# Moving the rearrangement of a latent convolution's data from its load and store to the producer's store and the consumer's load

## The chip, the cores and the metric

The kernel runs on one core of one Trainium2 chip. The metric is the device time of one execution in microseconds. TensorE (PE) multiplies matrices, VectorE (DVE), ScalarE (ACT) and GpSimd (POOL) work on tiles of 128 partitions, and SyncE (SP) issues all of this kernel's DMAs, in the order of one queue. Matrix products land in PSUM banks; everything between stages goes through DRAM buffers.

## The reference, cut to what matters

One layer of a backbone over 256 context tokens and 2048 latent tokens with 1024 channels. A normalised and modulated input is multiplied by one input projection. One part of its columns feeds a state-space scan; two others, `ga` and `gb`, feed the branch that matters here:

```python
def conformer_branch(ga, gb, conv_w, conv_b, ln_g, ln_b):
    h = ga * jax.nn.sigmoid(gb)
    h = depthwise_conv(h, conv_w, conv_b)   # 31 taps, per channel
    h = layer_norm(h, ln_g, ln_b)           # over the 1024 channels
    return jax.nn.silu(h)
```

The latent tokens lie on a grid of 32 rows by 64 columns, and the convolution runs along the rows (for each column and channel, 31 taps over 32 row positions). The context tokens are convolved along the sequence. Then `y_conf * silu(gsil)` and the scan's output are concatenated, multiplied by `w_out` (2048 x 1024), normalised, gated and added to the input.

## The kernel before, in words

The 2304 tokens are split in two halves (blocks of 256, 512, 512 and of 512, 512 tokens; block 0 is the context). All products are done three times with split operands (high times high, high times low, low times high), so TensorE has much to do. For each half the kernel runs, in this order: the columns of the scan's input (`xbc_phase`), then the units of `post`: eight `gab_unit`s, one for each group `j` of 128 channels, then the `silu_unit`s of the gates. Beside `post` run a scan over the tiles (`pass_a`) and, in the second half, the convolutions; generators are interleaved by hand (`interleave`, `merge`). On top of this a scheduler that simulates a time line lays out each engine's queue when the program is built, so the order within an engine need not be the written one; what is issued by one engine runs in its queue's order.

`gab_unit` makes `th`, the gated product of 128 channels by 256 or 512 tokens, in a buffer `ev` of which there are three, and stores it (L532) to `GL[j]`, one row a channel, token after token. Weights come through `next_w`, three units ahead.

`lat_conv` treats a group `j` of 128 channels. Its matmuls (L626) contract over 32 grid rows of 4 channels at once, so it wants the input as `x`: partition (channel mod 4, grid row), then channel group `g` and grid column. It loads that from `GL[j]` with four DMAs (L608), each run being 64 columns, 256 bytes. ScalarE expands the taps from `kd` into `kbuf` (`expand`, L614). VectorE gathers the result from PSUM into `vt` (named cvv in the profile; partition: one of two channel halves, grid column; then grid row and 64 channels). Two DMAs (L636) store it to `CVL`, one row a token, in runs of 64 channels, 256 bytes. There is one `x` buffer and one `vt` buffer.

The end of the kernel is the out-projection over 18 tiles of 128 tokens, latent tiles from the last to the first, then the two context tiles. For each tile: `conf_pre` (L1028) loads the convolution's result `n` (cn) of 128 tokens by 1024 channels (one buffer, L1030), takes the statistics (L1033) and normalises it; `conf_act` (L1041) transposes it on TensorE (L1049) and applies the activation; `ssd_pre` (L959) loads and combines the scan's parts (y, z, elb; L977 to L982), with GpSimd updating the carried state (L988, L989); `ssd_norm` and `ssd_scale` make its normalisation factor yr and yh, yl; `out_part` (L1069) runs 96 matmuls, and `finish` (L1085, L1089) scales the result, adds the input and stores it. The steps are written so that a tile's preparation lies between the matmuls of the tile before.

Of the kernel before, what the change touches and what calls it, by code (L numbers as in the profile page):

```python
# [17 lines left out]
P = 128  # L18
D = 1024
KT = D // P  # L20
NH = 16
HD = 64
NT = 18
NCTX = 2
LAT = 2048
# [42 lines left out]
def backbone_kernel(ctx, tc, xa, xt_in, cols, rows, wconv, conf_b, gp_row, bg_row, state0, w_mod, w_dt, w_in, w_out,  # L68
                    y_ctx, y_lat, new_state):
    nc = tc.nc  # L70
    V, S, G, T, DMA = nc.vector, nc.scalar, nc.gpsimd, nc.tensor, nc.sync
# [5 lines left out]
    def bank(tag, name):  # L77
        return psp.tile([P, 512], F32, tag=tag, name=name, bufs=3 if tag == "mm" else 5)

    def dram(name, shape):  # L80
        return drp.tile(shape, F32, tag=name, name=name)
# [1 line left out]
    XB = [dram(f"xb{h}", [NCT * P, n]) for h, n in ((0, N1), (1, N2))]  # L83
    HALO = dram("halo", [NCT, P, 130])
    ZS = [dram(f"zs{h}", [D, HT[h] * P]) for h in range(2)]
    GL = [dram(f"gl{j}", [P, NT * P]) for j in range(KT)]
    GS = [dram(f"gs{h}", [D, HT[h] * P]) for h in range(2)]
    CVC = dram("cvc", [NCTX * P, D])
    CVL = dram("cvl", [LAT, D])
    YP = [dram(f"yp{i}", [P, D]) for i in range(NT)]  # L90
    ST = [dram(f"st{i}", [P, D]) for i in range(NT)]
    LT = [dram(f"lt{h}", [HT[h] * 32, P]) for h in range(2)]
# [33 lines left out]
    def rstd_of(pool, ms, name):  # L126
        r = pool.tile([P, 1], F32, tag="rstd", name=name, bufs=4)
        G.tensor_tensor(r, ms, nhalf, ALU.pow)
        return r
# [39 lines left out]
    def ev(name):  # L169
        return evp.tile([P, 512], F32, tag="ev", name=name, bufs=3)  # L170
# [189 lines left out]
    def next_w():  # L360
        while len(wq) < 3 and wcols:
            wq.append(load_w(*wcols.pop(0)))
        return wq.pop(0)

    def mm_cm(ps, w, h):
        wh, wl = w
        hh, hl = h
        BN = hh.shape[2]
        for k in range(KT):
            T.matmul(ps[:, :BN], wh[:, k, :], hh[:, k, :], start=(k == 0), stop=False)  # L370
            T.matmul(ps[:, :BN], wh[:, k, :], hl[:, k, :], start=False, stop=False)  # L371
            T.matmul(ps[:, :BN], wl[:, k, :], hh[:, k, :], start=False, stop=(k == KT - 1))  # L372
            yield
# [146 lines left out]
    def gab_unit(half, j, hb):  # L520
        wb = next_w()
        wa = next_w()
        for b in ORDER[half]:
            BN, o = BNS[b], TOK[b]
            pg = bank("mm", f"gb{half}_{j}_{b}")
            yield from mm_cm(pg, wb, hb[b])
            th = ev(f"gth{half}_{j}_{b}")[:, :BN]
            S.activation(th, pg[:, :BN], AF.Tanh, scale=0.5)  # L528
            pa_ = bank("mm", f"ga{half}_{j}_{b}")
            yield from mm_cm(pa_, wa, hb[b])  # L530
            V.scalar_tensor_tensor(th, th, 1.0, pa_[:, :BN], ADD, MUL)  # L531
            DMA.dma_start(GL[j][:, o:o + BN], th)  # L532

    def silu_unit(half, c0, dst, j, hb, order=None):
        w = next_w()
# [36 lines left out]
    def ctx_conv(j, tile):  # L572
        g = tile(f"cg{j}")
        G.memset(g[:, 0:15], 0.0)
        G.memset(g[:, 271:286], 0.0)
        DMA.dma_start(g[:, 15:271], GL[j][:, 0:256])
        yield
        acc = g[:, 512:768]
        w0 = C_CONFW + j * CW
        V.tensor_scalar(acc, g[:, 0:256], cv[:, w0:w0 + 1], cfb2[:, j:j + 1], MUL, ADD)  # L580
        for t in range(1, CW):
            V.scalar_tensor_tensor(acc, g[:, t:t + 256], cv[:, w0 + t:w0 + t + 1], acc, MUL, ADD)  # L582
            if t % 3 == 0:
                yield
        ps = bank("ss", f"cps{j}")
        for t in range(2):
            T.transpose(ps[:, t * P:(t + 1) * P], acc[:, t * P:(t + 1) * P], ident)
        o = g[:, 768:1024]
        S.mul(o, ps[:, :256], 0.5)
        DMA.dma_start(CVC[:, j * P:(j + 1) * P].rearrange("(t p) c -> p t c", p=P),  # L590
                      o.rearrange("p (t c) -> p t c", c=P))
        yield


    def lat_conv(j, lp, kbuf):
        cbb = lp.tile([P, HD], F32, tag="cbb", name=f"cbb{j}", bufs=2)
        for h in range(2):
            c0 = j * P + h * 64
            DMA.dma_start(cbb[h * 64:(h + 1) * 64], conf_b[c0:c0 + 64].partition_broadcast(64))
        kd = lp.tile([P, 32, 32], F32, tag="kd", name=f"kd{j}", bufs=1)  # L600
        for c4 in range(4):
            src = bass.AP(tensor=wconv.tensor, offset=(j * 4 + c4) * 64 * 32, ap=[[32, 32], [1, 1024]])
            DMA.dma_start(kd[c4 * 32:(c4 + 1) * 32].rearrange("p r g -> p (r g)"), src)

        x = lp.tile([P, 32, 64], F32, tag="cx", name=f"cx{j}", bufs=1)
        src = GL[j][:, 256:].rearrange("(g c) (r w) -> c r g w", c=4, w=64)
        for c4 in range(4):
            DMA.dma_start(x[c4 * 32:(c4 + 1) * 32], src[c4])  # L608

        def expand(u):  # L610
            kt = kbuf[u % 2]
            for c4 in range(4):
                rs = slice(c4 * 32, (c4 + 1) * 32)
                S.copy(kt[rs, :, rs].rearrange("p (h q) r -> p h q r", h=2),  # L614
                       kd[rs].rearrange("p r (h u q) -> p u h q r", h=2, u=4)[:, u])

        vt = lp.tile([P, 32, HD], F32, tag="cvv", name=f"cvv{j}", bufs=1)
        yield
        expand(0)
        yield  # L620
        for u in range(4):
            kt = kbuf[u % 2]
            ps = bank("ss", f"cp{j}_{u}")
            for q in range(4):
                for h in range(2):
                    T.matmul(ps[h * 64:(h + 1) * 64, q * P:(q + 1) * P], x[:, h * 16 + u * 4 + q, :], kt[:, h * 4 + q, :],  # L626
                             start=True, stop=True)
            if u < 3:
                expand(u + 1)
            yield  # L630
            V.scalar_tensor_tensor(vt[:, ::-1, u * 16:(u + 1) * 16].rearrange("p r c -> p c r"),
                                   ps.rearrange("p (c r) -> p c r", r=32), 0.5,
                                   cbb[:, u * 16:(u + 1) * 16].unsqueeze(2).to_broadcast([P, 16, 32]), MUL, ADD)
        for h in range(2):
            c0 = j * P + h * 64
            DMA.dma_start(CVL[:, c0:c0 + 64].rearrange("(r w) c -> w r c", w=64), vt[h * 64:(h + 1) * 64])  # L636
        yield


# [222 lines left out]
    def post(half, nb):  # L862
        return chain([gab_unit(half, j, hb) for j in range(8)] + [silu_unit(half, Z0, ZS, j, hb) for j in range(8)]
                     + [silu_unit(half, GS0, GS, j, hb) for j in range(nb)])
# [31 lines left out]
    V.tensor_tensor(wd4[:, :, 1, :], wdr, wd4[:, :, 0, :].bitcast(F32), SUB)  # L896
    xbc_phase(0, first, hb, [hprep(2, hb), hprep(0, hb)], tails, dt_post(0))
    extra = chain([gate_rows()] + [ctx_conv(j, big) for j in range(4)])
    interleave(post(0, 6), merge(scan(range(9)), 68, extra, 9 + 4 * 13), 90 * 8)
    last = [silu_unit(0, GS0, GS, j, hb, (1, 2, 0)) for j in (6, 7)]  # L900
# [23 lines left out]
    blocks = post(1, 5)  # L924
    cg = lambda name: lp.tile([P, D], F32, tag="cg", name=name, bufs=2)
    extra = chain(f for j in range(4) for f in (lat_conv(2 * j, lp, kbuf), ctx_conv(j + 4, cg), lat_conv(2 * j + 1, lp, kbuf)))
    sc_ = scan(range(9, NT))
    run(take(blocks, 24))
# [98 lines left out]

    def conf_pre(i):  # L1028
        n = p2.tile([P, D], F32, tag="cn", name=f"cn{i}", bufs=1)
        DMA.dma_start(n, CVC[i * P:(i + 1) * P, :] if i < 2 else CVL[(i - 2) * P:(i - 1) * P, :])  # L1030
        bs = p2.tile([P, 12], F32, tag="bs", name=f"bs{i}", bufs=2)
        for h in range(2):
            V.bn_stats(bs[:, 6 * h:6 * h + 6], n[:, h * 512:(h + 1) * 512])  # L1033
        mv = p2.tile([P, 2], F32, tag="mv", name=f"mv{i}", bufs=2)
        V.bn_aggr(mv, bs)
        V.tensor_scalar(mv[:, 1:2], mv[:, 1:2], EPS, None, ADD)
        r = rstd_of(p2, mv[:, 1:2], f"cr{i}")
        V.tensor_scalar(n, n, mv[:, 0:1], r, SUB, MUL)
        return n
# [59 lines left out]
    i = order[0]  # L1099
# [9 lines left out]
    for b in range(2):  # L1109
        for n, u in enumerate(last):  # L1110
            run(take(u, 8))
            if b == 0 and n == 1:
                yr = ssd_norm(i, yz)
            if b == 1 and n == 0:
                ph_b[1].close()
                p2 = ph_1.enter_context(tc.tile_pool(name="p2", bufs=1))
                yh = ssd_scale(i, yr)
                nrm = conf_pre(i)
# [11 lines left out]
    for a, i in enumerate(order):  # L1130
# [10 lines left out]
        if not last:  # L1141
            n = conf_pre(nxt)
# [76 lines left out]
```

## Time and profile before

| | |
|---|---|
| Runs of the kernel before | 1885.21 us median of 3 (1884.33 to 1887.44) |
| Profiled execution | 1890.22 us, span 1888.5 us, 26833 instructions |
| Mean granted clock of TensorE | 0.989 |
| DMA | 375.29 MB, mean 199 GB/s; queue busy 63.9% of 16 engines' span |
| Packets under 512 bytes | 85206 of 290400 |

The profile is of one execution. An engine's busy time counts its instructions, not their waits. The chain of work is followed back from the last instruction, at each step to what released it. A row such as `PE ... [3.11 <-DMA cx<-gl]` says that the engine was idle 3.11 us before this instruction and what ended that. [...] The DMA share in a table by stage is the mean busy share of 16 DMA engines; it can exceed 1 where transfers overlap.

### The profile page before, as it was taken

Reading aid. Unit: us, or ns where it says so; the run is one execution under the profiler, and the core shown is the slowest. Engines: PE = TensorE matmul, PEld = TensorE weight load, DVE = VectorE, ACT = ScalarE, POOL = GpSimd, SP = SyncE. Lnnn points to the kernel's source line nnn. Section 1 sums busy time; section 2 is a strip of 40 time slices with the busy share of each in tenths; the row PEclk is TensorE's granted clock in tenths of the full one; section 3 lists DMA queues with packets and bytes.
Section 4 is the critical chain, followed back from the end, with each engine's and each line's share of the span. In section 5 each row is a group of like instructions: output and inputs, shape, how many; then the busy total and the mean of one; then the engine's idle time right before and its main releaser. Section 6 shows DMA issues by size and latency. Waiting matters only on the chain.

```text
span 1888.5 us, 26833 instructions
## 1 busy us (share of the span) xinstructions
PE 1827.4 (97%) x9739; PEld 1500.1 (79%) x9739; DVE 1192.4 (63%) x1699; ACT 839.9 (44%) x1786; POOL 264.6 (14%) x351
## 2 busy tenths in 40 slices
PE   7899999999999999999999998999999999999998
PEld 4788887787787888888877776767787888888886
DVE  2487877776545543586596758655438767776762
ACT  3647424443455441744356666664414323222321
POOL 0002001111111100100001111100003233333220
PEclk9999999999999999999999999999999999999999
DMA  8556665564686754445587888987887565555532
GB/s 299 213 199 214 216 217 187 169 219 154 206 274 222 229 204 162 162 154 198 186 184 220 213 228 226 246 213 201 248 262 237 182 183 168 160 171 168 177 104 75
DMA packets 290400, 375.29 MB, mean 199 GB/s; under 512 B 85206, under 2 KB 187478, under 8 KB 290268
## 3 DMA queue, kind: packets, MB, share of 16 engines
q1 hardware_dynamic: 290268, 373.58, 63.9%
q8 instruction: 77, 1.26, 0.3%
q14 instruction: 55, 0.45, 0.1%
HBM read 243.92 MB, written 129.59 MB: 198 GB/s over the span
## 4 chain that ended last, share of the span: by engine, by line
PE 60%; DMA 6%; issue 4%; ACT 3%; DVE 3%; SPq 1%; POOL 1%; POOLq 0%; DVEq 0%; ACTq 0%
PE op L1069 19%; PE sp L370 6%; PE sp L371 6%; PE sp L372 6%; DMA lb<-lt 4%; PE xp L372 2%; PE xp L371 2%; PE xp L370 2%; PE ga L370 1%; PE qo L976 1%; PE ga L372 1%; PE ga L371 1%; PE py L712 1%; PE gb L370 1%; PE gb L372 1%
## 5 line engine op out<-in xcount | busy, mean ns | idle before, releaser
L676 ACT ACTIVATE lb<-lb,WB 128x128 f32<-128x128 f32 x576 | 184.2, 391 | 150.9 <-POOL lb L668 149.0
L370 PE MATMUL sp<-hh,wh 128*128 128x512 f32 (+1 forms) x640 | 239.3, 374 | 1.9 <-DVE sth L542 1.9
L371 PE MATMUL sp<-hl,wh 128*128 128x512 f32 (+1 forms) x640 | 237.6, 371 | 0.0
L372 PE MATMUL sp<-hh,wl 128*128 128x512 f32 (+1 forms) x640 | 237.0, 370 | 0.0
L668 POOL TENSOR_SCALAR_AFFINE_SELECT lb<-lb 128x512 f32<-128x512 f32 x144 | 108.7, 759 | 751.8 <-ACT el L665 393.8
L370 PE MATMUL xp<-hh,wh 128*128 128x512 f32 (+1 forms) x480 | 178.0, 372 | 5.3 <-ACT wh L345 3.4
L371 PE MATMUL xp<-hl,wh 128*128 128x512 f32 (+1 forms) x480 | 178.2, 372 | 0.2 <-DVE hl L291 0.2
L372 PE MATMUL xp<-hh,wl 128*128 128x512 f32 (+1 forms) x480 | 178.1, 371 | 0.0
L467 DVE SCALAR_TENSOR_TENSOR cva<-raw,cwh,cva 128x1280 f32<-128x1280 f32 (+1 forms) x96 | 142.5, 1493 | 15.3 <-ACT cva L461 13.4
L370 PEld LDWEIGHTS sp<-hh,wh 128*128 128x128 f32 x640 | 121.1, 189 | 23.9 <-DVE sth L542 2.3
L372 PEld LDWEIGHTS sp<-hh,wl 128*128 128x128 f32 x640 | 121.1, 189 | 20.7 <-issue 0.2
L371 PEld LDWEIGHTS sp<-hl,wh 128*128 128x128 f32 x640 | 121.1, 189 | 20.3 <-issue 0.5
L370 PE MATMUL gb<-hh,wh 128*128 128x512 f32 (+1 forms) x320 | 121.5, 380 | 6.1 <-DVE gth L531 6.1
L370 PE MATMUL ga<-hh,wh 128*128 128x512 f32 (+1 forms) x320 | 120.2, 376 | 3.2 <-ACT gth L528 3.2
L371 PE MATMUL gb<-hl,wh 128*128 128x512 f32 (+1 forms) x320 | 119.4, 373 | 0.0
L372 PE MATMUL gb<-hh,wl 128*128 128x512 f32 (+1 forms) x320 | 119.3, 373 | 0.0
L372 PE MATMUL ga<-hh,wl 128*128 128x512 f32 (+1 forms) x320 | 118.3, 370 | 0.0
L371 PE MATMUL ga<-hl,wh 128*128 128x512 f32 (+1 forms) x320 | 118.2, 369 | 0.0
L582 DVE SCALAR_TENSOR_TENSOR cg<-cg,cv 128x256 f32<-128x256 f32 x240 | 112.3, 495 | 2.5
L542 DVE SCALAR_TENSOR_TENSOR sth<-sth,sp 128x512 f32<-128x512 f32 (+1 forms) x80 | 50.4, 630 | 96.0 <-ACT sth L541 96.0
L370 PEld LDWEIGHTS xp<-hh,wh 128*128 128x128 f32 x480 | 91.3, 190 | 22.0 <-ACT wh L345 4.1
L680 DVE TENSOR_TENSOR lb<-lb,lb 128x512 f32<-128x512 f32 x72 | 50.2, 697 | 88.6 <-ACT lb L676 55.8
(219 smaller groups left out, 3862.9 us busy)
## 6 DMA issues: line engine op xcount, KB each, us to landing
lb<-lt SPq DMA_DIRECT2D x144, 256.0 KB, 4.6
wr<-in_w_in SPq DMA_DIRECT2D x88, 256.0 KB, 4.9
whd<-wh SPq DMA_DIRECT2D x44, 512.0 KB, 3.2
wld<-wl SPq DMA_DIRECT2D x44, 512.0 KB, 4.6
wh<-whd SPq DMA_DIRECT2D x44, 512.0 KB, 5.7
wl<-wld SPq DMA_DIRECT2D x44, 512.0 KB, 5.6
xT<-xb SPq DMA_DIRECT2D x18, 512.0 KB, 5.6
yp<-yg SPq DMA_DIRECT2D x36, 256.0 KB, 4.8
```

Source lines behind the costliest of these rows:

```text
L370: T.matmul(ps[:, :BN], wh[:, k, :], hh[:, k, :], start=(k == 0), stop=False)
L371: T.matmul(ps[:, :BN], wh[:, k, :], hl[:, k, :], start=False, stop=False)
L372: T.matmul(ps[:, :BN], wl[:, k, :], hh[:, k, :], start=False, stop=(k == KT - 1))
L467: V.scalar_tensor_tensor(a[:, :n], raw[:, t:t + n], cwh[:, ct * 5 + t:ct * 5 + t + 1], a[:, :n], MUL, ADD)
L542: V.scalar_tensor_tensor(th, th, 1.0, ps[:, :BN], ADD, MUL)
L582: V.scalar_tensor_tensor(acc, g[:, t:t + 256], cv[:, w0 + t:w0 + t + 1], acc, MUL, ADD)
L668: G.affine_select(E[g, hq, d], E[g, hq, d], pattern=[[0, 4], [sg, P]], compare_op=ALU.is_ge, fill=NEG, base=0, channel_multiplier=-sg)
L676: S.activation(lb[:, h, :], lb[:, h, :], AF.Exp, bias=WB[:, i, c + h:c + h + 1])
L680: V.tensor_tensor(a, a, E[g, hq, 1], ADD)
L712: T.matmul(py[g][j * HD:(j + 1) * HD, q * P:(q + 1) * P], xt[g][:, h * HD:(h + 1) * HD], E[g, hq, 0][:, t, :], start=True, stop=True)
L976: T.matmul(po[:, q * P:(q + 1) * P], Sb[g][:, q * P:(q + 1) * P], ct[:, g, :], start=True, stop=True)
L1069: T.matmul(pso[n], lhs[:, k % 8, :], w[:, n * 512:(n + 1) * 512], start=(k == 0 and m == 0), stop=(k == 15 and m == 2))
```

## The change

The gated product is stored in the order in which the convolution reads it, and the convolution's result is stored as it lies in `vt`, to be gathered by the out-projection.

- `GL[j]` becomes two buffers: `GLC[j]` for the 256 context tokens, as before, and `GLX[j]`, one row of 8 KB for each partition of `x`.
- `gab_unit` stores block 0 with one DMA and every other block with four, one for each channel mod 4, each from 32 partitions (every fourth) in runs of 256 bytes.
- `lat_conv` loads `x` with one DMA in place of four, and stores `vt` with one in place of two, in rows of 8 KB.
- `CVL` becomes 1024 rows (channel group and half, grid column) of 2048 values (grid row, 64 channels). `conf_pre` loads a latent tile with two DMAs of 64 partitions, in runs of 256 bytes, in place of one with 4 KB rows. A tile of 128 tokens is two grid rows.

The arithmetic is not touched.

```diff
-    GL = [dram(f"gl{j}", [P, NT * P]) for j in range(KT)]
+    GLC = [dram(f"glc{j}", [P, NCTX * P]) for j in range(KT)]
+    GLX = [dram(f"glx{j}", [P, LAT]) for j in range(KT)]
-    CVL = dram("cvl", [LAT, D])
+    CVL = dram("cvl", [D, LAT])
...
-            DMA.dma_start(GL[j][:, o:o + BN], th)
+            if b == 0:
+                DMA.dma_start(GLC[j], th)
+                continue
+            r0 = (o - NCTX * P) // 64
+            for c4 in range(4):
+                DMA.dma_start(GLX[j][c4 * 32 + r0:c4 * 32 + r0 + BN // 64, :].rearrange("r (g w) -> g r w", w=64),
+                              th.rearrange("(g c) (r w) -> c g r w", c=4, w=64)[c4])
...
-        DMA.dma_start(g[:, 15:271], GL[j][:, 0:256])
+        DMA.dma_start(g[:, 15:271], GLC[j])
...
-        src = GL[j][:, 256:].rearrange("(g c) (r w) -> c r g w", c=4, w=64)
-        for c4 in range(4):
-            DMA.dma_start(x[c4 * 32:(c4 + 1) * 32], src[c4])
+        DMA.dma_start(x.rearrange("p g w -> p (g w)"), GLX[j])
...
-        for h in range(2):
-            c0 = j * P + h * 64
-            DMA.dma_start(CVL[:, c0:c0 + 64].rearrange("(r w) c -> w r c", w=64), vt[h * 64:(h + 1) * 64])
+        DMA.dma_start(CVL[j * P:(j + 1) * P, :], vt.rearrange("p r c -> p (r c)"))
...
-        DMA.dma_start(n, CVC[i * P:(i + 1) * P, :] if i < 2 else CVL[(i - 2) * P:(i - 1) * P, :])
+        if i < NCTX:
+            DMA.dma_start(n, CVC[i * P:(i + 1) * P, :])
+        else:
+            for e in range(2):
+                DMA.dma_start(n[e * 64:(e + 1) * 64, :].rearrange("w (j c) -> w j c", c=64),
+                              CVL.rearrange("(j w) (r c) -> r w j c", w=64, c=64)[2 * (i - NCTX) + e])
```

## Prediction

> **What bounds the kernel now.** I read the page's engine totals first, then a table by stage, then who stops TensorE in the one stage where it idles, then the out-projection's queue rows.
>
> ```profile
> PE 1827.4 (97%) x9739; PEld 1500.1 (79%) x9739; DVE 1192.4 (63%) x1699; ACT 839.9 (44%) x1786; POOL 264.6 (14%) x351
> 240.00:600.00 360.00, 348.80 (x1956) 289.72 (x1955) 236.57 (x413) 162.77 (x408) 39.73 (x63) 0.99 0.63 205
> 940.00:1400.00 460.00, 438.97 (x2550) 346.60 (x2550) 289.27 (x467) 261.68 (x577) 48.25 (x68) 0.98 0.83 227
> 1476.00:1780.00 304.00, 304.00 (x1490) 252.86 (x1489) 214.43 (x243) 88.33 (x186) 97.28 (x84) 1.00 0.57 173
> ```
>
> The first line is the page's total, the other three are stages (start and end, length, then busy time of TensorE, its weight loads, VectorE, ScalarE and GpSimd; granted clock, DMA share, GB/s). TensorE is busy 97% of the span. The change touches three stages. From 240 to 600 us the first half's gated blocks are stored; TensorE idles 11.2 us there. From 940 to 1400 us lies the latent convolution: TensorE idles 460 - 438.97 = 21.0 us and the DMA engines are at their highest share, 0.83. From 1476 to 1780 us the out-projection runs with TensorE at 304 of 304 us: nothing can be won there, only lost.
>
> In the convolution stage the chain of work and TensorE's rows with their idle time read:
>
> ```profile
> 1051.82 3.59 SPq L636
> 1055.46 2.06 SPq L608
> 1057.57 1.68 SPq L608
> 1059.34 2.04 SPq L656
> 1062.67 3.96 DMA lb<-lt
> 1072.99 1.09 PE cp L626 x16
> ...
> 1161.43 1.15 SPq L608 DMA_DIRECT2D cx<-gl  x2
> ...
> 1162.68 4.75 DMA lb<-lt
> 1178.73 1.97 PE cp L626 x16
> ...
> 1040.26 1.98 PE L626 MATMUL cp<-kbuf,cx 128*64 128x128 f32 x16 [4.12 <-ACT kbuf L614]
> 1072.99 1.09 PE L626 MATMUL cp<-kbuf,cx 128*64 128x128 f32 x16 [2.07 <-ACT kbuf L614]
> 1178.73 1.55 PE L626 MATMUL cp<-kbuf,cx 128*64 128x128 f32 x12 [2.68 <-ACT kbuf L614]
> 1260.06 1.90 PE L626 MATMUL cp<-kbuf,cx 128*64 128x128 f32 x16 [3.11 <-DMA cx<-gl]
> ```
>
> Read it backwards: TensorE idled 2.07 us before 1072.99 because ScalarE's expansion of the taps (L614) came late; ScalarE had waited for a decay row (lb), whose issue at 1059.34 stood in SyncE's queue behind the store of the conv result (L636, 3.59 us) and the loads of its input (L608, 2.06 and 1.68 us). The same before the stall of 2.68 us: lb's transfer at 1162.68 begins when two such loads (1161.43) have been issued; the stall of 3.11 us waits for the input load itself. So the convolution's two rearranging transfers clog the one DMA queue and reach TensorE three times.
>
> **The prices.**
>
> ```profile
> L532 SPq DMA_DIRECT2D gl<-gth x40: 319/324/4454, 246.4 to 1195.3; - x40
> L608 SPq DMA_DIRECT2D cx<-gl x32: 322/640/3267, 947.9 to 1292.7; - x32
> cvl<-cvv SPq DMA_DIRECT2D x16, 512.0 KB, 6.6
> cn<-cvl SPq DMA_DIRECT2D x16, 512.0 KB, 4.0
> 951.00:953.00 2.00, 2.00 (x10) 1.67 (x9) 2.00 (x5) 0.00 (x0) 0.00 (x0) 1.00 1.36 160
> 984.00:986.00 2.00, 1.27 (x9) 0.87 (x7) 2.00 (x5) 1.83 (x6) 0.00 (x0) 1.00 1.34 167
> 1529.00:1530.00 1.00, 1.00 (x6) 0.80 (x5) 0.00 (x0) 0.00 (x0) 0.00 (x0) 1.00 0.78 300
> ```
>
> Issue times are min/median/max in ns; the DMA rows give us to landing. Saturated, the input load in 256-byte pieces moves 160 GB/s (951 to 953), the result's store in 256-byte pieces 167 (984 to 986), and long rows 300 (1529, out-projection loads). The change keeps the number of 256-byte pieces (4096 a channel group on either side) and moves them: from the conv's load to the gated store, from the conv's store to the out-projection's load.
>
> **Part 1, input load of the conv.** Four loads become one of 8 KB rows: 1 MB takes 1048.6/300 = 3.5 us in place of 1048.6/160 = 6.6, and one issue replaces four of 0.64 us. Eight groups: -25 us of DMA time in the stage. **Part 2, result store.** Two become one: 3.5 for 1048.6/167 = 6.3 us, -22 us. With both, SyncE no longer stands still for 3.59 + 2.06 + 1.68 us before a decay row. I credit the three stalls whose chain the rows show: 2.07 + 2.68 + 3.11 = **-7.9 us**. Ends: 0, if something else on ScalarE is late at the same place, and -21.0, all the idle time of the stage. I take the value of the shown chains. Late next is the ordinary decay load, 4 to 5 us from issue.
>
> **Part 3, gated store.** Each of 32 blocks of 512 tokens is stored by four DMAs of 256-byte pieces instead of one of 2 KB rows; the 8 context blocks stay single. SyncE's issue grows from 0.32 to 4 x 0.32 = 1.3 us, at most 4 x 0.64 = 2.6; the transfer from 262/300 = 0.9 to 262/160 = 1.6 us. No new wait: the queue already stood at this place for VectorE's product. Behind it wait weight and decay loads, 1 to 2 us later, in a window with a DMA share of 0.63; the second half's 16 blocks add 16 x 0.7 = 12 us of transfers to the convolution stage, against 47 taken away. The product's buffer is held about 2 us longer, one of three. On TensorE: **0**, hidden by the weights fetched three units ahead; without that cover each block costs its 1 us of added issue, bounded above by as much idle time again as the window has, 11.2 us. A gain is excluded.
>
> **Part 4, the gather (L1030).** Two loads of 64 partitions in 256-byte pieces replace one with 4 KB rows. No row shows this read. At 160 GB/s 512 KB takes 524.3/160 = 3.3 us instead of 524.3/300 = 1.75: +1.5 us. Ends: 0 (a gain is excluded, as both rows with small pieces are slower) and +2.6, the landing of the result's store against that of the present load (6.6 - 4.0); I take the nearer row, the load at 160. The second issue is hidden, as the data queue behind y and z anyway. Who waits is VectorE, whose order is fixed when the program is built: the statistics of cn stand ahead of the next tile's work.
>
> ```profile
> 1582.39 1.29 DVE L1033 BATCH_NORM_STATS2 bs<-cn 128x6 f32<-128x512 f32 x2 [3.43 <-DMA cn<-cvl]
> 1589.41 1.65 DVE L1089 TENSOR_TENSOR o<-o,xr 128x1024 f32<-128x1024 f32 x1
> 1592.29 2.00 DVE L978 TENSOR_TENSOR y<-y,elb 128x1024 f32<-128x1024 f32 x1
> 1594.32 2.19 DVE L979 TENSOR_TENSOR y<-y,z 128x1024 f32<-128x1024 f32 x1
> 1599.58 1.22 DVE L1011 TENSOR_TENSOR yl<-y,yh 128x1024 fp32r<-128x1024 f32 x1
> 1607.91 0.70 DVE L1033 BATCH_NORM_STATS2 bs<-cn 128x6 f32<-128x512 f32 x1 [3.63 <-DMA cn<-cvl]
> ...
> 1575.92 0.38 SPq L1030 DMA_DIRECT2D cn<-cvl  x1
> 1600.83 0.32 SPq L966 DMA_DIRECT2D y<-yp  x1
> 1601.24 0.38 SPq L1030 DMA_DIRECT2D cn<-cvl  x1
> ...
> L979 DVE TENSOR_TENSOR y<-y,z x18: 1210/2193/2195, 1375.9 to 1818.4; 128x1024 f32<-128x1024 f32 x18
> L978 DVE TENSOR_TENSOR y<-y,elb x17: 1225/1998/2375, 1373.1 to 1816.7; 128x1024 f32<-128x1024 f32 x17
> L1089 DVE TENSOR_TENSOR o<-o,xr x17: 1215/1390/1992, 1469.1 to 1862.7; 128x1024 f32<-128x1024 f32 x17
> ...
> 1586.87 0.55 POOL L128 TENSOR_TENSOR yr<-yms,nhalf 128x1 f32<-128x1 f32 x1 [2.13 <-DVE oms L1079]
> 1593.62 0.38 PE L1003 MATMUL pm<-ident,yr 128*128 128x128 f32 x2
> ```
>
> This is a loop: statistics at 1582.39, VectorE nearly without a pause up to yl's end at 1600.80, which frees y's buffer, SyncE issues y, then cn at 1601.24, statistics again at 1607.91. The period is 1601.24 - 1575.92 = 25.32 us, TensorE's own. So a later cn comes back a tile later, and adds up unless VectorE can regain it. It can: three operations run at 1.65, 2.00 and 2.19 us where their shortest are 1.215, 1.225 and 1.210, because they run beside GpSimd's state update, which starts at TensorE's pace; VectorE moved later meets less of it, up to 0.44 + 0.78 + 0.98 = 2.2 us a tile. That is over 1.5, so the lag settles. The first to tell TensorE of a lag is yr, done at 1587.42 and used at 1593.62: 6.2 us of room. Even at +2.6 the excess of 0.4 over some 12 tiles makes 4.8 us, within it. Cost: **0**.
>
> [...]
>
> **Sum.** -7.9 + 0 + 0 = -7.9 us on a span of 1888.5: 1880.6. The profiled execution took 1890.22 us, 5.0 above the median of the runs, 1885.21. I apply the difference to the median: **1877.3 us**, -0.4%. A change within 0.2%, 3.8 us, is about what a measurement of this kernel cannot tell from none.
>
> **Rivals.** *No gain* (chance 0.20): the stalls only change their cause, since ScalarE is also held by GpSimd's masks, and the scheduler that lays out the queues orders them anew. For it: the stall of 4.12 us before 1040, no such transfer near. Against: the chain names L636 and L608. Only the wait for cx goes, -3.1 us, less some added issue: 1882 to 1887, say 1884. *The gather is slower than any 256-byte read here* (0.18; the other sign): it decides once its surcharge exceeds 2.2 us, a read above 1.75 + 2.2 = 3.95 us, or below 133 GB/s. For it: its pieces lie one new row of CVL apart, 8 KB, or 64 rows, 512 KB, which no row shows. Against: the result's store wrote pieces one old row, 4 KB, or 64 rows, 256 KB, apart at 167. At 85 GB/s, half that, it takes 6.2 us; the surcharge of 4.4 exceeds by 2.2 a tile, 12 tiles make 26 less the 6.2 - 2.2 = 4 us of room left, +22: 1899. [...] *The gated stores hold the queue* (0.12): 32 blocks x 1 us of issue, a third of it reaching TensorE, +11: 1888. Against: in the first half only 11.2 us of idle time exist at all. The *forecast* has 0.50, its own range 1867 to 1883 (a larger part of the 21.0 us below, half the credit above).
>
> **The numbers.** Faster by over 0.2% (below 1881.4): 0.47 of the forecast, 0.03 of no gain, 0.03 of the others: 0.53. Within: 0.02 + 0.15 + 0.04 = 0.21. Slower: the rest, 0.26. The range, 1867 to 1900, leaves out half of the slow gather and a little below.
>
> **What would show it.** Right: input loads of 1 MB at 3.5 to 5 us to landing; no SyncE issue of the conv's store above 2 us; DMA share from 940 to 1400 near 0.75; TensorE idle there near 13 us; statistics that start 1.5 us later against TensorE, L978 and L979 shorter, period still 25.3. Wrong: a period above 25.4 or TensorE waiting for yr (slow gather); stalls at L626 as before with lb still late (no gain); TensorE waiting more than 11 us between 240 and 600 (stores).

## The result: 1913.78 us, slower by 1.35%

| | before | after |
|---|---|---|
| Median of the runs | 1885.08 us (1884.33 to 1887.44) | 1913.78 us (1905.01 to 1916.37) |
| Ratio, 95% interval | | 1.0135 (1.0115 to 1.0154) |
| Profiled execution, span | 1890.22, 1888.5 us | 1905.01, 1903.3 us |
| Mean granted clock | 0.989 | 0.987 |
| First to last matmul of the out-projection | 1426.0 to 1880.2: 454.2 us | 1425.4 to 1895.3: 469.9 us |

The predicted 1877.3 us, and the range that ended at 1900, are missed on the slow side. The profiled execution of after was the fastest of its runs; its span is 14.8 us longer than that of before, and the last row shows where: the out-projection starts as early as before and takes 15.7 us more. These two traces do not hold the whole loss: the profiled execution of before lay 5.1 us above its median and that of after 8.8 us below, so 13.9 of the 28.7 us between the medians are not in them. The executions of after also had granted clocks of 0.982 to 0.987, those of before 0.983 to 0.992; what part of the loss goes with that was not separated. One execution of all, 2566.79 us at a granted clock of 0.656 in the gather half with the opened loop below, is left out of its ratio.

The page's engine line of after, and the same three stages as before (columns as in the prediction):

```profile
PE 1835.1 (96%) x9739; PEld 1501.2 (79%) x9739; DVE 1190.7 (63%) x1699; ACT 838.4 (44%) x1786; POOL 260.4 (14%) x351
...
240.00:600.00 360.00, 349.23 (x1949) 289.81 (x1947) 239.87 (x412) 162.96 (x408) 39.23 (x63) 0.99 0.65 206
940.00:1400.00 460.00, 441.01 (x2561) 346.44 (x2560) 291.07 (x467) 261.92 (x579) 54.27 (x68) 0.99 0.71 229
1476.00:1780.00 304.00, 297.26 (x1440) 244.89 (x1439) 192.98 (x228) 83.75 (x179) 78.76 (x78) 0.99 0.66 166
```

Three readings. The DMA engines' share in the convolution stage fell from 0.83 to 0.71, so the load did move; but TensorE idles 460 - 441.01 = 19.0 us there, against 21.0. The out-projection, full before, now has 6.7 us of gaps and 1440 instructions in place of 1490: 50 at 304/1490 = 0.204 us are 10.2 us of work not done in that window. The gaps explain 6.7 of these; the rest lies in instructions counted as busy, which the trace does not split further. The table of TensorE's waits (total, times, longest) names the gaps:

```profile
PE cp L631 <- ACT kbuf L619: 11.5, 5, 3.5
PE pm L1006 <- POOL yr L129: 9.6, 9, 2.8
PE cp L631 <- DVE cvv L636: 3.7, 1, 3.7
```

The second line is new: TensorE waits for yr nine times. Before, the out-projection had no such wait. The first line says that the convolution's waits for the expanded taps are what they were (12.0 us in 6 waits before); only the one wait for the input (3.11) is gone, and one of 3.7 us for cvv (third line; 0.5 before) has come in its place.

Now one tile of the out-projection after, from the engines' own rows (SPq: the DMA issues on SyncE's queue):

```profile
1571.17 0.49 PE L1006 MATMUL pm<-ident,yr 128*128 128x128 f32 x2 [1.19 <-POOL yr L129]
...
1556.83 0.32 SPq L969 DMA_DIRECT2D y<-yp  x1
1557.25 1.82 SPq L1037 DMA_DIRECT2D cn<-cvl  x2
1584.22 2.06 SPq L1037 DMA_DIRECT2D cn<-cvl  x2
...
1566.10 1.29 DVE L1041 BATCH_NORM_STATS2 bs<-cn 128x6 f32<-128x512 f32 x2 [7.32 <-DMA cn<-cvl]
1573.12 1.62 DVE L1097 TENSOR_TENSOR o<-o,xr 128x1024 f32<-128x1024 f32 x1
1575.96 2.27 DVE L981 TENSOR_TENSOR y<-y,elb 128x1024 f32<-128x1024 f32 x1
1578.26 1.22 DVE L982 TENSOR_TENSOR y<-y,z 128x1024 f32<-128x1024 f32 x1
1582.56 1.21 DVE L1014 TENSOR_TENSOR yl<-y,yh 128x1024 fp32r<-128x1024 f32 x1
1592.38 1.29 DVE L1041 BATCH_NORM_STATS2 bs<-cn 128x6 f32<-128x512 f32 x2 [6.61 <-DMA cn<-cvl]
...
1571.09 0.55 POOL L129 TENSOR_TENSOR or<-oms,nhalf 128x1 f32<-128x1 f32 x1
1571.60 2.05 POOL L991 TENSOR_TENSOR Sb<-Sb,eTb 128x512 f32<-128x512 f32 x2
1573.61 3.54 POOL L992 TENSOR_TENSOR Sb<-Sb,stl 128x512 f32<-128x512 f32 x2
```

and the same GpSimd operations before:

```profile
1587.39 0.55 POOL L128 TENSOR_TENSOR or<-oms,nhalf 128x1 f32<-128x1 f32 x1
1588.94 3.02 POOL L988 TENSOR_TENSOR Sb<-Sb,eTb 128x512 f32<-128x512 f32 x2 [1.00 <-PE qo L976]
1591.92 3.51 POOL L989 TENSOR_TENSOR Sb<-Sb,stl 128x512 f32<-128x512 f32 x2
```

This is the loop of the prediction, with its two sizes. From the issue of cn to the statistics it takes 1566.10 - 1557.25 = 8.85 and 1592.38 - 1584.22 = 8.16 us, where before it was 1607.91 - 1601.24 = 6.67: 1.5 to 2.2 us more. From statistics to the end of yl, VectorE needs 1582.56 + 1.21 - 1566.10 = 17.67 us, against 1600.80 - 1582.39 = 18.41: 0.74 us less. The period is 1592.38 - 1566.10 = 26.28 us against 25.32. VectorE regains one of the three overlaps (L982, now 1.22, starts at 1578.26, behind the update's end at 1573.61 + 3.54 = 1577.15; before, L979 started at 1594.32 and the update ended at 1595.43) and keeps the others (L981 2.27, L1097 1.62). The GpSimd rows say why: its update stands in its queue behind "or", which needs VectorE's oms. Before, it then waited 1.00 us for TensorE's qo; after, it starts without a pause, 5.50 us behind the statistics in both tiles (1571.60 - 1566.10 and 1597.88 - 1592.38), so it now moves with VectorE and the overlap with it.

### The profile page after: what moved, and what is told of

Same layout as the page of the kernel before. It is cut to its first block, busy times and chain, and to the rows that moved or that the text cites. A ratio compares the mean times of both kernels' runs of the same rounds, so it can differ in the third digit from the quotient of the medians.

```text
span 1903.3 us, 26978 instructions
## 1 busy us (share of the span) xinstructions
PE 1835.1 (96%) x9739; PEld 1501.2 (79%) x9739; DVE 1190.7 (63%) x1699; ACT 838.4 (44%) x1786; POOL 260.4 (14%) x351
## 4 chain that ended last, share of the span: by engine, by line
PE 45%; DMA 11%; DVE 10%; issue 5%; ACT 3%; POOL 2%; SPq 1%; POOLq 0%; DVEq 0%; ACTq 0%
PE sp L371 6%; PE sp L372 6%; PE sp L373 6%; PE op L1077 5%; DMA cn<-cvl 4%; DMA lb<-lt 4%; PE xp L372 2%; PE xp L373 2%; PE xp L371 2%; PE py L715 1%; DVE y L981 1%; PE gb L371 1%; PE ga L371 1%; PE gb L372 1%; PE cp L631 1%
## 5 line engine op out<-in xcount | busy, mean ns | idle before, releaser
L671 POOL TENSOR_SCALAR_AFFINE_SELECT lb<-lb 128x512 f32<-128x512 f32 x144 | 114.0, 798 | 736.0 <-ACT el L668 366.7
L468 DVE SCALAR_TENSOR_TENSOR cva<-raw,cwh,cva 128x1280 f32<-128x1280 f32 (+1 forms) x96 | 142.7, 1495 | 14.8 <-ACT cva L462 12.9
L983 ACT ACTIVATE z<-y 128x1024 f32<-128x1024 f32 x18 | 19.1, 1061 | 223.6 <-DVE y L982 223.6
```

Of the source, the lines that this page charges most:

```text
L468: V.scalar_tensor_tensor(a[:, :n], raw[:, t:t + n], cwh[:, ct * 5 + t:ct * 5 + t + 1], a[:, :n], MUL, ADD)
L671: G.affine_select(E[g, hq, d], E[g, hq, d], pattern=[[0, 4], [sg, P]], compare_op=ALU.is_ge, fill=NEG, base=0, channel_multiplier=-sg)
L983: S.activation(z, y, AF.Square)
```

## The experiments

The runs of before beside them had medians of 1884.71 to 1885.72 us; each ratio is to those on the same chip.

**One half at a time.** The first kernel keeps the gated store and the input load of the change, and the result's store and load of before:

```diff
-    CVL = dram("cvl", [D, LAT])
+    CVL = dram("cvl", [LAT, D])
...
-        DMA.dma_start(CVL[j * P:(j + 1) * P, :], vt.rearrange("p r c -> p (r c)"))
+        for h in range(2):
+            c0 = j * P + h * 64
+            DMA.dma_start(CVL[:, c0:c0 + 64].rearrange("(r w) c -> w r c", w=64), vt[h * 64:(h + 1) * 64])
```

> The store half alone: gated product stored in the order of use and loaded with long rows; the convolution's result is stored and loaded as before. Theory L (the loss is the loop statistics - yl - y's load - gather in the out-projection, which the gather's 1.5 us push over TensorE's 25.3 us a tile): no wait for yr, cn 6.3 to 6.7 us from issue to statistics, 1882 to 1888 us. Rival S (the 96 added store issues on SyncE's queue make the loss): 1900 us or more, TensorE's idle time from 940 to 1400 us well above 21. Rival O (the scheduler's new order of the queues): anywhere, also with slower tiles of 26 us.

Measured: 1893.68 us (1891.99 to 1895.88), ratio 1.0049 (1.0031 to 1.0067). The out-projection is full again, without a wait for yr. So the store half alone loses 8.7 us, before the gather comes into it. Neither expectation held: the time lies between the two, and TensorE's idle time from 940 to 1400 us, 18.8 us, did not rise above 21.

The second is the other half: gather as in the change, `GL` as before.

```diff
-            for c4 in range(4):
-                DMA.dma_start(GLX[j][c4 * 32 + r0:c4 * 32 + r0 + BN // 64, :].rearrange("r (g w) -> g r w", w=64), ...
+            DMA.dma_start(GL[j][:, o:o + BN], th)
...
-        DMA.dma_start(x.rearrange("p g w -> p (g w)"), GLX[j])
+        src = GL[j][:, 256:].rearrange("(g c) (r w) -> c r g w", c=4, w=64)
+        for c4 in range(4):
+            DMA.dma_start(x[c4 * 32:(c4 + 1) * 32], src[c4])
```

> The gather half alone: result stored as it lies and gathered by the out-projection; the gated product is stored and loaded as before. Theory L: the whole loss is here, tiles of 26 to 27 us, TensorE waiting for yr in 8 to 13 tiles, 1900 to 1916 us. Rival S: 1880 to 1888.

Measured: 1898.51 us (1897.31 to 1904.50), ratio 1.0080 (1.0057 to 1.0103). Its out-projection starts earlier (1416.0) and takes 473.8 us:

```profile
PE pm L1001 <- POOL yr L128: 12.8, 11, 3.7
```

The two losses, 0.49% and 0.80%, add up to the whole within the intervals. There are two causes.

**The loop of the out-projection.** A second buffer for the gathered tile, `bufs=2` for cn:

> The whole change with two buffers for cn in place of one, so that a tile's gather can start a tile earlier. Theory L: the statistics no longer wait for the gather, the period is back at 25.3 us, no wait for yr, 1882 to 1888 us. Rival D (the gather simply loads the DMA engines too much): VectorE still waits 6 us for cn, 1900 or more.

Measured: 1910.85 us, ratio 1.0140 (1.0121 to 1.0159), waits for yr 12.4 us. No help: the engines' order stayed, y then cn on SyncE, and VectorE still met the statistics of the tile just loaded at the same place; the second buffer was used to run a whole tile earlier, not to wait less. The rival's number came, but not its reason: the runs with the opened loop, below, gather as much and keep TensorE full.

GpSimd's update of the state left out of the out-projection (that part of the computation is missing; `pass` for L991 and L992):

> The whole change without GpSimd's update of the carried state in the out-projection (that part of the computation is left out). Theory L: L981, L982 and L1097 run at 1.2 us each in place of 2.27, 1.22 and 1.62, so the loop is 1.5 us shorter and, with 26.3 - 1.5 = 24.8 below 25.3, TensorE sets the pace: no wait for yr, 1884 to 1892 us. If GpSimd does not matter for the loop: tiles stay at 26 us or more and the time at 1905 to 1916.

Measured: 1899.88 us (1898.26 to 1905.16), ratio 1.0078 (1.0058 to 1.0099); no wait for yr. Without the update VectorE's two operations run at their short times:

```profile
1555.99 1.23 DVE L981 TENSOR_TENSOR y<-y,elb 128x1024 f32<-128x1024 f32 x1
1557.26 1.23 DVE L982 TENSOR_TENSOR y<-y,z 128x1024 f32<-128x1024 f32 x1
1570.97 1.29 DVE L1040 BATCH_NORM_STATS2 bs<-cn 128x6 f32<-128x512 f32 x2 [2.16 <-DMA cn<-cvl]
```

Here VectorE has the room that the prediction gave it, and its waits for the gather shrink, from some 7 us to 2.16 in this row. The time did not come down to the level of the store half: at the start of the stage one wait of 6.9 us of TensorE for zr is left.

Then the loop opened by order: the tile is loaded one tile ahead, and its statistics are tied behind pl, so that SyncE issues cn no longer right behind y:

```diff
-    def conf_pre(i):
-        n = p2.tile([P, D], F32, tag="cn", name=f"cn{i}", bufs=1)
+    def conf_load(i):
+        n = p2.tile([P, D], F32, tag="cn", name=f"cn{i}", bufs=2)
...
-        V.tensor_tensor(pl, v, ph.bitcast(F32), SUB)
+        tie[0] = V.tensor_tensor(pl, v, ph.bitcast(F32), SUB)
...
-            n = conf_pre(nxt)
+            with tc.issue_after(tie[0]):
+                n = conf_pre(nxt, nl)
+            if a + 2 < NT:
+                nl = conf_load(order[a + 2])
```

On the full change:

> The full change with the same opened loop: the gathered tile is loaded one tile ahead into a second buffer and its statistics stand behind pl. Theory L: the period of the out-projection goes back to 25.3 us and its length from 469.9 to about 455, so 1893 to 1897 us, the level of the store half alone (1893.7), since the cost of the gated store's issues stays. Rival M (DMA contention): 1908 to 1914 us, as the full change.

Measured: 1895.44 us (1894.52 to 1902.85), ratio 1.0065 (1.0044 to 1.0086). On the gather half alone:

> The gather half alone (the convolution's result stored as it lies, gathered by the out-projection; the gated product stored as before), with the out-projection's loop opened: the result's tile is loaded one tile ahead into a second buffer, and its statistics stand behind pl, the last VectorE step of the tile's normalisation, so that SyncE no longer issues it behind y. Theory L (the loop of statistics, yl, y, result load, landing, statistics had 0.74 us of room and the gather asks 1.5): the period goes back to TensorE's 25.3 us, no wait of TensorE for yr, out-projection about 454 us where the gather half alone has 473.8, and the convolution stage keeps its gain of some 10 us, so 1876 to 1884 us, at or under the kernel before. Rival M (the 256-byte reads take DMA time from y, z, the outputs and the weights, and the wait for yr is only where it shows): the loads are as many and as long, so out-projection stays at 468 to 474 and the time at 1894 to 1900 us.

Measured: 1883.02 us, ratio 0.9985 (0.9973 to 0.9997). On the kernel before, as a control:

> The kernel before with the opened loop alone: the convolution's result loaded one tile ahead into a second buffer, its statistics behind pl; no part of the change. Theory L: the loop had 0.74 us of room there and TensorE never waited in it, so no change, 1882 to 1888 us, and what the gather half and the full change gain with the opened loop is the layouts' own. Rival: the opened loop is a gain by itself, 1876 to 1881 us, and the layouts bring nothing.

Measured: 1883.26 us, ratio 0.9992 (0.9978 to 1.0006). The opened loop removes what the gather half cost (1.0080 to 0.9985) and does nothing measurable to the kernel before. TensorE's out-projection stage of the full change with the opened loop:

```profile
1476.00:1780.00 304.00, 304.00 (x1490) 252.84 (x1489) 197.86 (x242) 86.51 (x180) 102.52 (x84) 1.00 0.69 173
```

It is full, with a higher DMA share than after (0.69 against 0.66): the reads themselves cost TensorE nothing; the place of their wait did.

**What makes the gather land late.** Half of each tile gathered, half read as long rows:

> The full change with half the dose: 64 of the 128 partitions of each latent tile are gathered in 256-byte pieces, the other 64 come as long rows from elsewhere in the result, so that half of each tile holds other data. Theory L has a threshold: half the surcharge, 0.75 us, is about the 0.74 us of room, so the period is 25.3 to 25.6 us, the out-projection 455 to 459 and the time 1895 to 1900 us. Rival M (cost in proportion to the 256-byte pieces read): half of 15.7 us is left, 1903 to 1906 us.

Measured: 1911.73 us, ratio 1.0144 (1.0126 to 1.0162). Both expectations failed: half the short pieces cost the whole. So the loss does not go with the number of short pieces, and four more loads in the gather's place, which bring other data than the tile should hold, took it apart:

```diff
 one load, rows of 4 KB:
+            DMA.dma_start(n, CVL[(i - NCTX) // 2 * P:((i - NCTX) // 2 + 1) * P, (i - NCTX) % 2 * D:((i - NCTX) % 2 + 1) * D])
 two loads of 64 partitions, rows of 4 KB:
+            for e in range(2):
+                DMA.dma_start(n[e * 64:(e + 1) * 64, :], CVL[(i - NCTX) * 64:(i - NCTX + 1) * 64, e * D:(e + 1) * D])
 one load of 128 partitions in 256-byte pieces (q, s: quotient and rest of (i - NCTX) by 2):
+            DMA.dma_start(n.rearrange("p (j c) -> p j c", c=64),
+                          CVL[q * P:(q + 1) * P, :].rearrange("p (r s c) -> p s r c", s=2, c=64)[:, s])
 two loads of 128 partitions, half the columns each:
+            for e in range(2):
+                DMA.dma_start(n[:, e * 512:(e + 1) * 512], CVL[q * P:(q + 1) * P, s * D + e * 512:s * D + (e + 1) * 512])
```

> The full change with the gather replaced by one load a tile of 128 rows of 4 KB from the same stored result (other data than the tile should hold). Theory P (the surcharge of the gather is its 256-byte pieces) and theory T (it is the two DMAs a tile, each to 64 partitions, in place of one to 128) both say: issue to statistics back at 6.3 to 6.7 us, period 25.3, no wait for yr, 1893 to 1897 us, the level of the store half alone. If it stays at 1908 or more, neither is right, and the surcharge comes from where or when the result lies.

> The full change with the gather replaced by two loads a tile, each of 64 rows of 4 KB to 64 partitions (other data than the tile should hold): no 256-byte piece, but two DMAs. Theory P: as with one load, period 25.3, 1893 to 1897 us. Theory T: issue to statistics 8.2 to 8.6 us as in the full change and in its half dose, period 26.2, 1906 to 1914 us.

> The full change with the gather replaced by one DMA a tile to 128 partitions in 256-byte pieces, every second piece of an 8 KB row (other data than the tile should hold): all pieces short, but one DMA. Theory P: issue to statistics 8.2 to 9 us, period 26.2, waits for yr, 1906 to 1914 us. Theory T: period 25.3 and 1893 to 1898 us.

> The full change with the gather replaced by two DMAs a tile, each to all 128 partitions in rows of 2 KB, half the columns each (other data than the tile should hold). If the number of DMAs is the cause: issue to statistics 7.5 us or more, period above 25.5, 1900 to 1910 us, as with two loads of 64 partitions (1903.7). If it is the 64 partitions of each: issue to statistics 6.8 us or less, period 25.3, 1890 to 1896 us, as with one load (1892.0).

| in place of the gather | issue to statistics, median (range) of 11 tiles | out-projection | median us | ratio (95%) |
|---|---|---|---|---|
| one load, 128 partitions, 4 KB rows | 4.5 (3.9 to 4.9) | 454.3 | 1891.97 | 1.0032 (1.0018 to 1.0045) |
| one load, 128 partitions, 256-byte pieces | 6.6 (6.4 to 6.8) | 455.1 | 1895.17 | 1.0044 (1.0029 to 1.0060) |
| two loads, 128 partitions, 2 KB rows | 5.5 (5.1 to 5.9), second half 7.3 (6.8 to 7.7) | 456.4 | 1895.40 | 1.0048 (1.0032 to 1.0065) |
| two loads, 64 partitions, 4 KB rows | 8.0 (7.1 to 9.0) | 467.6 | 1903.65 | 1.0085 (1.0062 to 1.0108) |
| the change (two, 64, 256 bytes) | 8.2 (7.8 to 9.4) | 469.9 | 1913.78 | 1.0135 (1.0115 to 1.0154) |

In the first row cn is issued 1.6 us after y, in the others 0.4 us, so only the others are to be compared with the kernel before, 6.5 us (6.1 to 6.8) over the same tiles. The rows behind the table, one tile each; two loads of 64 partitions:

```profile
1533.78 1.10 SPq L1037 DMA_DIRECT2D cn<-cvl  x2
...
1541.89 1.29 DVE L1040 BATCH_NORM_STATS2 bs<-cn 128x6 f32<-128x512 f32 x2 [6.55 <-DMA cn<-cvl]
1547.40 2.05 POOL L991 TENSOR_TENSOR Sb<-Sb,eTb 128x512 f32<-128x512 f32 x2
```

one load in 256-byte pieces:

```profile
1530.46 0.56 SPq L1037 DMA_DIRECT2D cn<-cvl  x1
...
1537.22 1.29 DVE L1041 BATCH_NORM_STATS2 bs<-cn 128x6 f32<-128x512 f32 x2 [3.97 <-DMA cn<-cvl]
1543.22 2.04 POOL L991 TENSOR_TENSOR Sb<-Sb,eTb 128x512 f32<-128x512 f32 x2 [0.47 <-PE qo L979]
```

two loads of all partitions:

```profile
1531.79 0.86 SPq L1038 DMA_DIRECT2D cn<-cvl  x2
...
1537.32 0.69 DVE L1041 BATCH_NORM_STATS2 bs<-cn 128x6 f32<-128x512 f32 x1 [5.97 <-DMA cn<-cvl]
1539.05 0.69 DVE L1041 BATCH_NORM_STATS2 bs<-cn 128x6 f32<-128x512 f32 x1
```

8.11 and 6.76 us; with two loads of all partitions the statistics end 1539.05 + 0.69 - 1531.79 = 7.95 us after the issue, as before (6.67 + 1.29 = 7.96). So the number of DMAs is not the cause, and 256-byte pieces alone add some 0.1 us. Loads that reach 64 partitions each bring the loop and the waits for yr (8.2 us in 5) back by themselves. By the medians of the runs they go from 1.0044 and 1.0048, the two rows with the same issue distance, to 1.0085, roughly half of the way to 1.0135; by the out-projection of the profiled executions they go most of it (467.6 of 469.9 us), so how the loss is shared stays open. The rest needs 64 partitions and short pieces together. Two things in it were not run by themselves: the gather's pieces lie up to 512 KB apart, those of the one load 512 bytes; and its two issues last longer, 1.82 us in the rows of after above against 1.10 here. The GpSimd rows mark the switch: with a wait for qo left (0.47) the period is TensorE's, 25.3 us; without one it is the loop's.

Why a load that reaches 64 partitions lands later, no run shows. What the runs show is the size: from issue to statistics a median of 8.0 us with long rows against 6.5 before, the second issue included.

**The store half.** One DMA a block in place of four, the pieces the same, in another order:

```diff
-            for c4 in range(4):
-                DMA.dma_start(GLX[j][c4 * 32 + r0: ... ].rearrange("r (g w) -> g r w", w=64), ... [c4])
+            DMA.dma_start(GLX[j].rearrange("(r a) (q w) -> r (a q) w", a=4, w=64)[r0:r0 + BN // 64].rearrange("r p w -> p r w"),
+                          th.rearrange("p (r w) -> p r w", w=64))
```

> The store half alone, with each block's gated product stored by one DMA of 256-byte pieces in place of four; the bytes, the pieces and the region of memory stay, but the pieces lie in another order, so the convolution reads other data than it should. Theory S (the store half's loss is SyncE's time: four issues of 0.64 us a block hold the loads of the decays and weights behind them): the loss of 8.8 us goes to most of its part, 1883 to 1888 us, and no run of issues at the gated store above 1 us. Rival P (the loss is the 256-byte pieces themselves on the DMA engines, where long rows were before): 1892 to 1896 us as the store half, whatever the number of issues.

Measured: 1888.04 us, ratio 1.0010 (0.9997 to 1.0022), against 1.0049 with four. The pieces and bytes are as many; the issues are not. SyncE's queue in the changed kernel, just after 1098 us, then all its issues of the gated store and of the decay rows (min/median/max in ns), and what the decay rows' issues waited for from 940 to 1400 us (total, times, longest):

```profile
1098.82 2.55 SPq L538 DMA_DIRECT2D glx<-gth  x4
1101.47 0.55 SPq L659 DMA_DIRECT2D lb<-lt  x1
1107.03 0.33 SPq L659 DMA_DIRECT2D lb<-lt  x1
...
L538 SPq DMA_DIRECT2D glx<-gth x128: 577/610/1722, 246.8 to 1199.2; - x128
L659 SPq DMA_DIRECT2D lb<-lt x144: 319/382/1407, 151.7 to 1290.5; - x144
SPq L659 <- DVE lb L683: 39.6, 16, 4.9
```

and of the kernel with one issue:

```profile
L537 SPq DMA_DIRECT2D glx<-gth x32: 360/371/4407, 248.4 to 1196.0; - x32
```

Four issues take 4 x 0.61 = 2.4 us and more a block. The decay rows behind them are not slow to issue, 1.4 us at most: between the two shown here the queue stood until VectorE had freed a decay row's buffer. TensorE's waits for the expanded taps do not follow the issues either: 12.0 us in the convolution stage with four, 12.0 with one, 12.2 with the four on ScalarE's queue, in the last run of this part. What the traces show is a sum. The out-projection starts at 1426.7 us in the store half, at 1425.4 to 1431.7 in the nine versions with both changed stores and the four issues on SyncE's queue, at 1420.9 to 1426.0 in three executions with the convolution of before, at 1422.6 with one issue, and at 1419.1 and 1418.6 with the four on ScalarE's queue. One place can be read, in the changed kernel:

```profile
1136.47 0.41 DVE L587 TENSOR_SCALAR cg<-cg,cv,cfb 128x256 f32<-128x256 f32 x1 [5.45 <-DMA cg<-glc]
```

VectorE stood for the context convolution's input, whose load SyncE issued at 1134.37; behind it in VectorE's order came the gathering of cvv that TensorE waited for (3.7 us, above). This wait for cvv is there in all nine of those versions, 3.2 to 5.5 us, and in no other above 1.2. By which waits the rest of the cost reaches TensorE stays open.

At last the four issues were moved to ScalarE's queue, without and with the opened loop:

```diff
-                DMA.dma_start(GLX[j][c4 * 32 + r0: ...
+                nc.scalar.dma_start(GLX[j][c4 * 32 + r0: ...
```

> The full change with the four issues of each gated block moved from SyncE's queue to ScalarE's, and nothing else. Theory: the two losses add, so the gain of some 14 us that this move brought with the opened loop (1895.4 to 1880.5) comes here too, 1894 to 1900 us, with the waits for yr and the period of 26.2 us still there. Rival: the move takes effect only with the loop open, 1904 to 1914 us.

Measured: 1901.70 us (1892.38 to 1904.68), ratio 1.0075 (1.0047 to 1.0104); the waits for yr are there (9.3 us in 8).

> The full change with the opened loop (1895.4 us) and the four issues of each gated block moved from SyncE's queue to ScalarE's. Theory S (the store half loses by SyncE's issue time): SyncE's decay and weight loads are no longer held, the convolution's stalls after 1100 us shrink, 1884 to 1890 us; ScalarE pays 128 issues of about 0.3 to 0.6 us, which must stay beside TensorE. Rival: ScalarE's expansion of the taps and its tanh are held by the issues instead, and TensorE waits for kbuf and gth: 1895 to 1905 us.

Measured: 1880.50 us (1875.69 to 1884.08), ratio 0.9973 (0.9959 to 0.9987). The pieces and the partitions of each store are as before the move, so it is the issues in SyncE's queue that cost. Both causes gone, the version gains 0.27%, the best of the study. How much of that is the layouts' own is not shown: the opened loop alone stood at 0.9992 (0.9978 to 1.0006), which overlaps, and no run moved the gated store of the kernel before to ScalarE's queue. Its convolution stage idles 16.0 us:

```profile
940.00:1400.00 460.00, 444.02 (x2572) 348.91 (x2571) 289.71 (x468) 261.54 (x579) 47.87 (x69) 0.99 0.70 227
```

The DMA share is 0.70 in the convolution stage, against 0.73 with the opened loop alone; the time went from 1895.44 to 1880.50 us.

**A second execution of the kernel before:**

> The kernel before, unchanged, for a second trace: 1882 to 1890 us, and in the trace the same three stalls of the convolution on x, 11 us of waits on kbuf in its stage, and an out-projection without waits.

Measured: 1886.32 us, span 1884.6. Its waits in the convolution, and the stage:

```profile
PE cp L626 <- ACT kbuf L614: 7.4, 4, 3.0
PE cp L626 <- DMA cx<-gl: 2.7, 1, 2.7
...
940.00:1400.00 460.00, 441.84 (x2563) 349.43 (x2562) 289.03 (x468) 260.62 (x576) 49.30 (x69) 0.98 0.83 226
```

The stage idles 460 - 441.84 = 18.2 us with 7.4 us of kbuf waits, against 21.0 and 12.0 in the execution that the prediction was made from. A third, the kernel before with the opened loop, whose convolution is the same, idles 17.5 us there with 11.1 us of kbuf waits.

## Why the prediction was wrong, step by step

- **Parts 1 and 2, -7.9 us: the mechanism is right, the size wrong.** The rearranging transfers do leave the queue: the DMA share fell to 0.71 and no issue of the result's store is above 0.4 us. But the stage's idle time fell by 2.0 us in the change, and by 1.5 to 5.0 us (17.5, 18.2 or 21.0 to 16.0) once the other losses were out of the way. The credit took three stalls of one execution as if each had one cause. Ahead of the 2.68 us stall SyncE's queue in the kernel before reads `1156.93 4.45 SPq L532 DMA_DIRECT2D gl<-gth  x1`, then the two input loads' 1.15 us: most of that delay was a gated store, which the change makes four, and not the rearranging loads. And in a second execution of the same kernel 4.6 of the 12.0 us of kbuf waits were not there, and in all versions some 7 to 13 us of such waits stay; what makes the decay row late there is not shown. That is the rival *no gain*, in part. The 1 MB input loads land in 6.4 and 7.4 us, the two whose landing the trace has, not in 3.5 to 5.
- **Part 3, 0 us: failed.** The step that failed is that the added issues are hidden by weights fetched ahead. The issue was 0.61 us each, near the upper end given (2.6 us a block; its 16 x 0.7 = 12 us of transfers is 11.2, on which nothing hangs), and the store half cost 8.7 us, near the rival *the gated stores hold the queue* (+11). One issue a block left 0.10% of the 0.49%; the four on another queue took 12 to 15 us off (1913.78 to 1901.70, 1895.44 to 1880.50). So the term put at nothing was issue time in the shared queue; one wait that goes with it could be read, for cvv, the rest could not.
- **Part 4, 0 us: failed, at the regain.** The surcharge of 1.5 us was about right (1.5 to 2.2), but not for the reason given: 256-byte pieces alone cost 0.1, loads of 64 partitions some 1.5 with long rows and 1.7 with short ones, by the medians. The step that failed is "which starts at TensorE's pace": 2.2 us a tile were to be regained, 0.74 was. GpSimd's update waited only 1.00 us for TensorE (0.6 to 1.4 over the stage); moved by more than that, it goes with VectorE. Its queue was not looked at, only its effect on VectorE. The loss is 15.7 us in the profiled execution, and the loop, yr as the first to tell TensorE and the line "wrong if TensorE waits for yr" were right.
- **The rival of the other sign** had the right place and consequence, with a threshold of 2.2 us in place of about 1 and a rate (85 GB/s) that no run showed; what the runs showed is a gathered tile in use 8.2 us after its issue in the median, against 6.5 before.
- **The correction for the execution**, 5.0 us taken off a profiled time above the median, should also have warned that part of the stalls seen in it belonged to it.

## What to carry to other kernels

When a wait lies on a loop through a DMA and back, the room may be a small wait of an engine in the loop's wake, here GpSimd's 1.00 us for qo, and not the sum of the overlaps that a shift might undo: read the queue of the engine that causes the overlap. Count DMA instructions, not only bytes: four issues in place of one on a shared queue (a ratio of 1.0049 against 1.0010) and loads that reach half the partitions each (8.0 us from issue to statistics against 6.5) cost more here than short pieces alone (6.6 us). A stall seen once in one execution is worth less than its length: the waits for the expanded taps took 12.0 us in one execution of the kernel before and 7.4 in another.

## What was not expected of the hardware

- Two loads of 64 partitions with 4 KB rows were usable 7.1 to 9.0 us after their issue, one of 128 after 6.1 to 6.8 (512 KB a tile); two loads of 128 partitions cost nothing (7.95 us to the end of the statistics, 7.96 with one).
- Reading 512 KB to 128 partitions in 256-byte pieces took 6.4 to 6.8 us from issue to use, as with 4 KB rows (6.1 to 6.8): the 160 GB/s of the convolution's input load, four DMAs of 32 partitions each, was no measure for it.
- An issue of a gated piece store took 0.61 us in the median, against 0.37 for the same pieces in one DMA, four times as large.
